# Where the GELU of a hybrid layer is evaluated: in the SSM's output stage or in the last stage

## The chip, the cores and the metric

The kernel runs on one core of one Trainium2 chip. The metric is the device time of one execution in microseconds; the median of three runs of the kernel before is 1507.56 us (1506.02 to 1509.1). Engines are called by their names in the profile: PE multiplies matrices, DVE, ACT and POOL work on tiles element by element, and DMAs are issued from the queues of ACT and SP.

## The reference, cut to what matters

```
h = rms_norm(x, norm_gain)                       # x: 1 x 2048 x 1024
q, k, v, z_attn, u_ssm, z_ssm, g = split(h @ w_in)
attn = windowed_gqa(q, k, v, ...) * silu(z_attn)
y = s5_bidirectional(u_ssm, ...)                 # 2048 x 512, 32 groups of 16 channels
y = gelu(y)                                      # 0.5*y*(1+tanh(0.79788*(y+0.044715*y^3)))
y = y * sigmoid(y @ w_glu + b_glu)
ssm = y * silu(z_ssm)
merged = sigmoid(g_attn) * (attn @ w_branch_attn) + sigmoid(g_ssm) * (ssm @ w_branch_ssm)
out = rms_norm(x + merged @ w_out, final_norm_gain)
```

## The kernel before

Every product of two fp32 matrices is done as three matmuls: each operand is split into a high part (ACT copies it to the matmul's rounded fp32) and a low part (the difference, on DVE or POOL), and high x high, low x high and high x low are added up in PSUM (`mm3`, L220 to L222). A weight tile of 128 columns comes from HBM on SP's queue (`raw`), ACT makes its high part `wh` (L163) and POOL its low part `wl` (L155).

The program has three long stretches. **The in-projections** run over blocks of 512 tokens (`BLK`), one output tile of 128 channels x 512 tokens at a time (24 matmuls over the 1024 inputs), from 25 us to 1064 us. Between their matmuls a second stream of work, the generator `chain()`, is advanced: `mm3` calls `tick()` and `turn()`, and these give the generator credit by a rate, so that it takes about 1.2 steps for each tick (`RATE2`). `chain()` first does the SSM in 8 frames of 64 channels each (`frame(i)`, from about 190 to 660 us), then the attention (to about 1005 us), and at its end prepares the last stage: `gelu_prep` of the first block (about 1020 to 1051 us), `attn_prep`, and two loads. **The last stage** (1064 to 1507 us) takes the blocks in the order 2, 3, 1, 0 (`BO`): `glu` (the product with w_glu), `branch` (the two branch products, sixteen `mm3` of 12 matmuls), `outp` (the output projection). While a branch runs, `gelu_prep` of the next block is advanced by one step for each tick.

Each engine executes its own instructions in the order in which the program issues them, and an instruction that waits holds up all behind it on its engine; a DMA issued from ACT's queue stands in ACT's order too. No table or planner sets this order: it is the order in which Python calls are made, with two delays: `later(n, f)` runs f at the n-th tick from now, and `store` puts a DMA off to the second flush, a tick later than the next one.

In a frame, `emit(i, half)` (L893 to L913) forms y for 32 channels x 2048 tokens in one PSUM tile: the matmuls of L901 need the low part `Ml` (DVE, L749), those of L905 the low part `Hl` of the states (DVE, L891). Then ACT copies the PSUM tile to `Y` (L909) and two stores put it into `yS` in HBM. Around it stand the tiles for the next frame: `U0l`, `U1l` (the split inputs, L749, needed by the matmuls of L858), `wo` (L692 to L694), `Z` (L831), and `rt`, `X` of the rotation (L867 to L870).

`gelu_prep(b, lag)` loads for each of 4 channel tiles e a 128 x 512 piece of `yS` into `yt` (L1423, on ACT's queue) and then does five instructions over four steps: Square on ACT (L1429, it reads the tile with a stride and writes it in token order), (1+s)*y on DVE (L1433), tanh on ACT (L1437), (1+t)*y on DVE (L1441) with the high part `gh` on ACT (L1442), and the low part `gl` on DVE (L1446). Tiles 0 and 1 are loaded at the start, tile 2 and 3 one step ahead of the Square that reads them. `glu` needs `gh` and `gl`.

Of the kernel before, what the change touches and what calls it, by code (L numbers as in the profile page):

```python
# [7 lines left out]
F32 = mybir.dt.float32  # L8
# [3 lines left out]
AF = mybir.ActivationFunctionType  # L12
ALU = mybir.AluOpType
# [5 lines left out]
D = 1024  # L19
KD = 8  # L20
BLK = 512
NBLK = 4
COL_Q, COL_K, COL_V, COL_ZA, COL_U, COL_ZS, COL_G = 0, 512, 640, 768, 1280, 1792, 2304
G, P, C, T = 32, 64, 16, 8
M = S // T
GB = 4
# [6 lines left out]
GELU_Q = 0.044715 ** 0.5  # L33
# [4 lines left out]
def kernel(  # L38
# [10 lines left out]
    V, A, Q, PE = nc.vector, nc.scalar, nc.gpsimd, nc.tensor  # L49
# [6 lines left out]
    def scratch(name, shape):  # L56
        if dbg and name in dbg:
            return dbg[name]
        return dram.tile(shape, F32, name=name)

    uS = scratch("uS", [512, T, M])
    yS = scratch("yS", [512, T, M])
# [15 lines left out]
    stg = h_pool.enter_context(tc.tile_pool(name="stg", bufs=4))  # L78
# [3 lines left out]
    def bank(tag):  # L82
        return ps.tile([128, 512], F32, tag=tag, name=tag, bufs=PSB[tag])
# [3 lines left out]
    def store(dst, src):  # L87
        stores.append((1, dst, src))
# [8 lines left out]
        stores[:] = keep  # L97

    HALF = "half"
    sides = []  # L100
    laters = []

    def later(n, f):
        laters.append((n, f))
# [10 lines left out]
    def turn():  # L115

        for sd in sides:
# [3 lines left out]
            while sd["credit"] > 0.0:  # L121
                try:
                    sd["credit"] -= 0.5 if next(sd["gen"]) is HALF else 1.0
                except StopIteration:
# [544 lines left out]
    def ssm(pool):  # L669
# [95 lines left out]
        def chan(t, g):  # L765

            return bass.AP(tensor=t.tensor, offset=t.offset + g * C * T * M, ap=[[M, T], [T * M, C], [1, M]])
# [125 lines left out]
        def emit(i, half):  # L893
            s = st[i]
            H = s["H"][0]
            pt = bank("s1")
            for j in range(2):
                g = half * 2 + j
                o = pt[:, j * M:(j + 1) * M]
                for m, (a, b) in enumerate(((0, 0), (0, 1), (1, 0))):  # L900
                    PE.matmul(o, s["M"][a][:, g], s["U"][half][b][:, j], start=m == 0, stop=False)  # L901
                for n in range(2):
                    for m, (a, b) in enumerate(((0, 0), (0, 1), (1, 0))):
                        w = s["ws"][n][a][:, g].rearrange("p j c -> p (j c)")
                        PE.matmul(o, w, H[b][:, j, n], start=False, stop=n == 1 and m == 2)  # L905
                if j == 0:
                    yield
            Y = stg.tile([128, BLK], F32, tag="st", name="Y")
            A.activation(Y, pt, AF.Copy)  # L909
            for j in range(2):  # L910
                store(chan(yS, i * GB + half * 2 + j), Y[:, j * M:(j + 1) * M])

        def frame(i):  # L913

# [48 lines left out]
            yield from slot()  # L963
            yield from slot()
            yield from emit(i, 0)
            yield from slot()
            high_h(i, 1)
# [5 lines left out]
            if nx:  # L973
                prep_o(nx, V)
                split_u(nx, 0)
            yield from slot()
            yield from emit(i, 1)
            if nx:
                split_u(nx, 1)
# [47 lines left out]
    def attention(pool, order):  # L1027
# [173 lines left out]
        for i in range(NU + 3):  # L1201
            u0, u1, u2 = unit(i), unit(i - 1), unit(i - 2)
            for m in range(6):
# [37 lines left out]
                if end is not None:  # L1241
                    end()
                yield HALF


    with tc.manual_schedule():
# [133 lines left out]
        def chain():  # L1380
            with tc.tile_pool(name="sp", bufs=1) as sp:
                yield from ssm(sp)
            prm_pool.close()
            with tc.tile_pool(name="ap", bufs=1) as ap:
                yield from attention(ap, order)
            open_final()
            yield from gelu_prep(BO[0], 0)
            yield from attn_prep(BO[0], 0)
            load_zs(BO[0], 0)
            load_zs(BO[0], 1)  # L1390


        GC = 0.7978845608028654
        fin = {}

        def open_final():
# [7 lines left out]
        def ftile(shape, dt, tag, name, bufs=1):  # L1404
            return fin["fp"].tile(shape, dt, tag=tag, name=name, bufs=bufs)
# [7 lines left out]
        gx, ax, sx, mx = {}, {}, {}, {}  # L1413

        def gelu_prep(b, lag):
            gx[b] = [ftile([128, 4, BLK], F32R, t, t) for t in ("gh", "gl")]
            gh, gl = gx[b]
            tl = {}

            def ld(e):  # L1420
                t = ftile([128, D], F32, "xr", "yt", 3)
                y = t[:, 0:BLK].rearrange("p (j m) -> p j m", j=T)
                A.dma_start(out=y, in_=yS[e * 128:(e + 1) * 128, :, b * 64:(b + 1) * 64])  # L1423
                ta = t[:, BLK:D]
                tl[e] = (y.rearrange("p j m -> p m j"), ta, ta.rearrange("p (m j) -> p m j", j=T))

            def g0(e):
                yv, ta, tav = tl[e]
                A.activation(tav, yv, AF.Square, scale=GELU_Q)  # L1429

            def g1(e):
                yv, ta, tav = tl[e]
                V.scalar_tensor_tensor(tav, tav, 1.0, yv, ALU.add, ALU.mult)  # L1433

            def g2(e):
                yv, ta, tav = tl[e]
                A.activation(ta, ta, AF.Tanh, scale=GC)  # L1437

            def g3(e):
                yv, ta, tav = tl[e]  # L1440
                V.scalar_tensor_tensor(tav, tav, 1.0, yv, ALU.add, ALU.mult)  # L1441
                A.activation(gh[:, e], ta, AF.Copy)  # L1442

            def g4(e):
                yv, ta, tav = tl.pop(e)
                V.tensor_tensor(gl[:, e], ta, gh[:, e].bitcast(F32), ALU.subtract)  # L1446

            def g12(e):
                g1(e)
                g2(e)  # L1450

            steps = (g0, g12, g3, g4)
            ld(0)
            ld(1)
            for _ in range(1 + lag):
                yield
            for k in range(13):
                for s_ in range(3, -1, -1):
                    e, r = divmod(k - s_, 3)
                    if r == 0 and 0 <= e < 4:  # L1460
                        steps[s_](e)
                yield
                if k in (4, 7):
                    ld((k - 4) // 3 + 2)

        def attn_prep(b, lag):
            ax[b] = [ftile([128, 4, BLK], F32R, t, t) for t in ("ah", "al")]
# [216 lines left out]
        for i, b in enumerate(BO):  # L1684
            nxt = BO[i + 1] if i + 1 < NBLK else None
            if nxt is not None:
                sg = add_side(gelu_prep(nxt, 1), 1.0)
            branch(b, nxt)
            if nxt is not None:
                drain(sg)  # L1690
            load_xr(b, 0, A)
            if nxt is not None:
                glu(nxt)
                sa = add_side(attn_prep(nxt, 1), 1.0)
            outp(b, nxt is None)
            if nxt is not None:
                drain(sa)
# [48 lines left out]
```

## Time and profile before

| what | value |
|---|---|
| median of the runs | 1507.56 us |
| the profiled execution's own time | 1508.19 us |
| span of the profile | 1506.4 us |
| busy: PE / DVE / ACT / POOL | 94% / 69% / 44% / 42% of the span |
| granted clock of PE, mean | 0.979 of full speed |

The profiled execution took 0.63 us more than the median, and 1.8 us of its time lie outside the span. PE is the engine with the least idle time: 1418.1 of 1506.4 us. A time of the whole can change only where PE stands still, or where it runs at the lower clock, or where PE is not the engine that ends last. The waits of PE, by the instruction that ended them, are therefore the first view to read; then, for each, what the engine that ended the wait had been doing. A figure in brackets at the end of a row of the timeline is the idle time of that engine just ahead of the instruction, with what ended it. Idle time of an engine other than PE is room that further work can fill.

### The profile page before, as it was taken

To read this page: it belongs to the slowest core of one execution; us is meant where nothing else is said; L and a number is where in the kernel's file an instruction comes from. 1 tells how busy PE (TensorE), PEld (TensorE's weight loads), DVE (VectorE), ACT (ScalarE), POOL (GpSimd) and SP (SyncE) were. 2 spreads that over 40 slices of the span, in tenths; PEclk is the share of its full clock that TensorE was granted. 3 is DMA by queue.
4 is the path that set the end of the run, shared out by engine and by line. 5 is a ranking of instruction groups with operands and counts; after the bars stand their busy time and mean duration, and the time that the engine had idled before them with its cause. 6 is when DMAs were issued, how large, how long until landed. Compare 5 with 4: busy or idle time off the path is not lost.

```text
span 1506.4 us, 19697 instructions
## 1 busy us (share of the span) xinstructions
PE 1418.1 (94%) x6933; PEld 1154.6 (77%) x6933; DVE 1041.8 (69%) x1954; ACT 659.9 (44%) x1213; POOL 637.9 (42%) x683
## 2 busy tenths in 40 slices
PE   7999779899999999899999999999988999999998
PEld 6787567777778777788888888888766877877886
DVE  2327977779788788647999998874577386385442
ACT  6332133433534444535666666754453243242111
POOL 5520187758678777622111111112376153252320
PEclk9999989989999999999999999999999999999999
DMA  8534222322332332554333333235776375375441
GB/s 264 157 98 95 64 81 72 100 91 76 113 105 88 109 105 88 152 175 127 92 91 92 101 96 91 90 102 148 211 212 193 98 196 181 114 182 166 117 122 70
DMA packets 240723, 185.47 MB, mean 123 GB/s; under 512 B 57921, under 2 KB 202433, under 8 KB 240625
## 3 DMA queue, kind: packets, MB, share of 16 engines
q10 hardware_dynamic: 118192, 107.89, 24.3%
q1 hardware_dynamic: 122432, 76.34, 17.1%
q8 instruction: 54, 0.88, 0.2%
q14 instruction: 45, 0.36, 0.1%
HBM read 126.56 MB, written 57.62 MB: 122 GB/s over the span
## 4 chain that ended last, share of the span: by engine, by line
PE 39%; DVE 26%; issue 7%; DMA 6%; ACT 5%; POOL 4%; ACTq 1%; DVEq 0%; POOLq 0%; SPq 0%
PE pj L220 7%; PE pj L222 7%; PE pj L221 7%; PE s L1592 3%; PE s L1593 3%; PE s L1594 3%; DVE Hl L891 2%; DMA yt<-yS 2%; DVE X L879 2%; PE s L1163 2%; DVE X L868 2%; PE s L1110 2%; DVE rt L867 2%; DVE X L870 2%; PE s L1147 2%
## 5 line engine op out<-in xcount | busy, mean ns | idle before, releaser
L155 POOL TENSOR_TENSOR wl<-raw,wh 128x256 fp32r<-128x256 f32 x380 | 355.0, 964 | 573.5 <-ACT wh L163 483.7
L220 PE MATMUL pj<-hh,wh 128*128 128x512 f32 x976 | 391.2, 401 | 0.0
L222 PE MATMUL pj<-hh,wl 128*128 128x512 f32 x976 | 385.7, 395 | 0.0
L221 PE MATMUL pj<-hl,wh 128*128 128x512 f32 x976 | 385.6, 395 | 0.0
L222 PEld LDWEIGHTS pj<-hh,wl 128*128 128x128 f32 x976 | 185.6, 190 | 41.0
L220 PEld LDWEIGHTS pj<-hh,wh 128*128 128x128 f32 x976 | 186.3, 191 | 34.0
L221 PEld LDWEIGHTS pj<-hl,wh 128*128 128x128 f32 x976 | 186.1, 191 | 34.3
L163 ACT ACTIVATE wh<-raw 128x1024 fp32r<-128x1024 f32 x96 | 100.7, 1051 | 23.4 <-DMA raw<-in_w_branch_ssm_dram 7.9
L1592 PE MATMUL s<-woh,mh 128*128 128x512 f32 x256 | 102.3, 400 | 6.7 <-DVE xr L1599 6.7
L1594 PE MATMUL s<-woh,ml 128*128 128x512 f32 x256 | 102.0, 398 | 0.0
L1593 PE MATMUL s<-wol,mh 128*128 128x512 f32 x256 | 101.9, 398 | 0.0
L1127 ACT ACTIVATE p<-p,sml 128x384 f32<-128x384 f32 (+1 forms) x128 | 75.8, 594 | 16.3 <-DVE sml L1123 16.1
L1636 POOL TENSOR_TENSOR sm<-sm,mhalf 128x1 f32<-128x1 f32 x15 | 8.3, 550 | 170.1 <-DVE sm L1635 133.4
L404 ACT ACTIVATE st<-pj,bg 128x512 f32<-128x512 f32 x64 | 43.8, 685 | 79.0 <-PE pj L222 69.3
L1111 DVE CUSTOM_DVE_ANT_0 p<-s,bias 128x384 f32<-128x384 f32 (+1 forms) x128 | 68.3, 535 | 13.7 <-PE s L1110 13.2
L1599 DVE TENSOR_TENSOR xr<-xr,s 128x512 f32<-128x512 f32 x32 | 21.9, 686 | 69.3 <-PE s L1594 69.3
L867 DVE TENSOR_TENSOR rt<-X,es 128x1020 f32<-128x1020 f32 x32 | 43.3, 1353 | 38.1 <-issue 14.4
L1152 DVE TENSOR_TENSOR pl<-s,ph 128x512 fp32r<-128x512 f32 x92 | 62.9, 683 | 4.2 <-ACT ph L1150 2.9
L1110 PE MATMUL s<-kst,qs 128*128 128x384 f32 (+1 forms) x256 | 65.7, 339 | 0.0
L1592 PEld LDWEIGHTS s<-woh,mh 128*128 128x128 f32 x256 | 48.5, 189 | 20.5 <-DVE xr L1599 8.9
L870 DVE TENSOR_TENSOR X<-X,rt 128x510 f32<-128x510 f32 x64 | 62.0, 1009 | 1.1
L891 DVE TENSOR_TENSOR Hl<-X,Hh 64x1024 fp32r<-64x1024 f32 x32 | 46.7, 1460 | 17.9 <-ACT Hh L886 17.4
(307 smaller groups left out, 3049.2 us busy)
## 6 DMA issues: line engine op xcount, KB each, us to landing
raw<-in_w_in_dram SPq DMA_DIRECT2D x59, 512.0 KB
gS<-st ACTq DMA_DIRECT2D x64, 256.0 KB
gt<-gS ACTq DMA_DIRECT2D x64, 256.0 KB
x<-in_x_dram SPq DMA_DIRECT2D x16, 512.0 KB
raw<-in_w_branch_attn_dram SPq DMA_DIRECT2D x32, 256.0 KB
raw<-in_w_branch_ssm_dram SPq DMA_DIRECT2D x32, 256.0 KB
out_dram<-xr ACTq DMA_DIRECT2D x15, 512.0 KB
xr<-in_x_dram SPq DMA_DIRECT2D x12, 512.0 KB
```

The source lines that it names most:

```text
L155: eng.tensor_tensor(lo[:, ks], r[:, ks], hi[:, ks].bitcast(F32), ALU.subtract)
L163: A.activation(res[0], r, AF.Copy)
L220: PE.matmul(pt, w[0][:, k], r[0][:, k], start=start and k == 0, stop=False)
L221: PE.matmul(pt, w[0][:, k], r[1][:, k], start=False, stop=False)
L222: PE.matmul(pt, w[1][:, k], r[0][:, k], start=False, stop=stop and k == kt - 1)
L870: V.tensor_tensor(X[:, :, r], X[:, :, r], t[:, :, r], ALU.add if r == back else ALU.subtract)
L891: V.tensor_tensor(H[1][rows], xv, H[0][rows].bitcast(F32), ALU.subtract)
L1110: PE.matmul(pt[:, 0:w], s["qs"][:, h], kst[:, r, kv, k0 * 128:k1 * 128], start=r == 0, stop=r == 1)
L1127: A.activation(p[:, h, 0:w], p[:, h, 0:w], AF.Exp, bias=nm[:, j:j + 1], accum_out=den[:, j:j + 1])
L1592: PE.matmul(pt, mh[k][:, ts_], wo[0, n][:, k], start=k == 0, stop=False)
L1593: PE.matmul(pt, mh[k][:, ts_], wo[1, n][:, k], start=False, stop=False)
L1594: PE.matmul(pt, ml[k][:, ts_], wo[0, n][:, k], start=False, stop=k == KD - 1)
```

## The change

`emit` now evaluates the GELU's body on its contiguous tile: beside the copy to `Y`, ACT squares the PSUM tile into a second tile `th` (from the pool of two that the projections' tanh uses too); one tick later DVE forms (1+s)*y (`poly`), at the next tick ACT the tanh, at the third DVE (1+t)*y (`put`), and then the two stores are put off as before, so they are issued three ticks later than before. `gelu_prep` keeps the load, the split into `gh` (ACT) and `gl` (DVE), which now read the loaded tile with a stride in and out, and drops Square, the two DVE instructions and tanh. It has five steps instead of thirteen; in the branches (`lag` of 1) each step lasts two ticks. Tiles 2 and 3 are now loaded directly ahead of the step that copies them.

```
--- before.py
+++ after.py
@@ -97,6 +97,7 @@
         stores[:] = keep
 
     HALF = "half"
+    GC = 0.7978845608028654
     sides = []
     laters = []
 
@@ -906,9 +907,21 @@
                 if j == 0:
                     yield
             Y = stg.tile([128, BLK], F32, tag="st", name="Y")
+            ta = stg.tile([128, BLK], F32, tag="th", name="th", bufs=2)
             A.activation(Y, pt, AF.Copy)
-            for j in range(2):
-                store(chan(yS, i * GB + half * 2 + j), Y[:, j * M:(j + 1) * M])
+            A.activation(ta, pt, AF.Square, scale=GELU_Q)
+
+            def poly():
+                V.scalar_tensor_tensor(ta, ta, 1.0, Y, ALU.add, ALU.mult)
+
+            def put():
+                V.scalar_tensor_tensor(Y, ta, 1.0, Y, ALU.add, ALU.mult)
+                for j in range(2):
+                    store(chan(yS, i * GB + half * 2 + j), Y[:, j * M:(j + 1) * M])
+
+            later(1, poly)
+            later(2, lambda: A.activation(ta, ta, AF.Tanh, scale=GC))
+            later(3, put)
 
         def frame(i):
 
@@ -1390,7 +1403,6 @@
             load_zs(BO[0], 1)
 
 
-        GC = 0.7978845608028654
         fin = {}
 
         def open_final():
@@ -1413,6 +1425,7 @@
         gx, ax, sx, mx = {}, {}, {}, {}
 
         def gelu_prep(b, lag):
+
             gx[b] = [ftile([128, 4, BLK], F32R, t, t) for t in ("gh", "gl")]
             gh, gl = gx[b]
             tl = {}
@@ -1421,47 +1434,25 @@
                 t = ftile([128, D], F32, "xr", "yt", 3)
                 y = t[:, 0:BLK].rearrange("p (j m) -> p j m", j=T)
                 A.dma_start(out=y, in_=yS[e * 128:(e + 1) * 128, :, b * 64:(b + 1) * 64])
-                ta = t[:, BLK:D]
-                tl[e] = (y.rearrange("p j m -> p m j"), ta, ta.rearrange("p (m j) -> p m j", j=T))
-
-            def g0(e):
-                yv, ta, tav = tl[e]
-                A.activation(tav, yv, AF.Square, scale=GELU_Q)
-
-            def g1(e):
-                yv, ta, tav = tl[e]
-                V.scalar_tensor_tensor(tav, tav, 1.0, yv, ALU.add, ALU.mult)
-
-            def g2(e):
-                yv, ta, tav = tl[e]
-                A.activation(ta, ta, AF.Tanh, scale=GC)
-
-            def g3(e):
-                yv, ta, tav = tl[e]
-                V.scalar_tensor_tensor(tav, tav, 1.0, yv, ALU.add, ALU.mult)
-                A.activation(gh[:, e], ta, AF.Copy)
-
-            def g4(e):
-                yv, ta, tav = tl.pop(e)
-                V.tensor_tensor(gl[:, e], ta, gh[:, e].bitcast(F32), ALU.subtract)
-
-            def g12(e):
-                g1(e)
-                g2(e)
-
-            steps = (g0, g12, g3, g4)
+                tl[e] = y.rearrange("p j m -> p m j")
+
+            def chunks(t, e):
+                return t[:, e].rearrange("p (m j) -> p m j", j=T)
+
             ld(0)
             ld(1)
             for _ in range(1 + lag):
                 yield
-            for k in range(13):
-                for s_ in range(3, -1, -1):
-                    e, r = divmod(k - s_, 3)
-                    if r == 0 and 0 <= e < 4:
-                        steps[s_](e)
+            for k in range(5):
+                if k < 4:
+                    A.activation(chunks(gh, k), tl[k], AF.Copy)
+                if k > 0:
+                    V.tensor_tensor(chunks(gl, k - 1), tl.pop(k - 1), chunks(gh, k - 1).bitcast(F32), ALU.subtract)
                 yield
-                if k in (4, 7):
-                    ld((k - 4) // 3 + 2)
+                if lag:
+                    yield
+                if 0 < k < 3:
+                    ld(k + 1)
 
         def attn_prep(b, lag):
             ax[b] = [ftile([128, 4, BLK], F32R, t, t) for t in ("ah", "al")]
```

The instructions of PE, POOL and SP stand in the same order as before. On ACT, at the end of the chain (the last in-projections, `gelu_prep` of block 2; `st` and `gS` are those projections' outputs, `wh` the next weights), there stood before:

```order
L1423 DMA yt<-yS 128x8x64 x2
L404 ACTIVATE st<-pj,bg_91 128x512
L1429 ACTIVATE yt<-yt 128x512
L1437 ACTIVATE yt<-yt 128x512
L94 DMA gS<-st 128x512
L1442 ACTIVATE gh<-yt 128x512
L404 ACTIVATE st<-pj,bg_91 128x512
L1429 ACTIVATE yt<-yt 128x512
L163 ACTIVATE wh<-raw 128x1024 x2
L1437 ACTIVATE yt<-yt 128x512
```

And in the same place of ACT's order now (line numbers have moved by one to thirteen):

```order
L1436 DMA yt<-yS 128x8x64 x2
L405 ACTIVATE st<-pj,bg_91 128x512
L1448 ACTIVATE gh<-yt 128x512 x2
L94 DMA gS<-st 128x512
L1436 DMA yt<-yS 128x8x64
L1448 ACTIVATE gh<-yt 128x512
L405 ACTIVATE st<-pj,bg_91 128x512
L1436 DMA yt<-yS 128x8x64
L1448 ACTIVATE gh<-yt 128x512
L164 ACTIVATE wh<-raw 128x1024 x2
L94 DMA gS<-st 128x512
```

The two `wh` copies stood behind the copy and the Square of the first two tiles; now they stand behind all four `gh` copies and behind two loads, each with the copy that reads it right after it.

On DVE, in frame 2 of the SSM, between the low parts of the states (`Hl`) and of the next frame's inputs (`U0l`), there stood before:

```order
L401 SCALAR_TENSOR_TENSOR st<-th,pj 128x512 x2
L891 TENSOR_TENSOR Hl<-X,Hh 64x1024 x2
L401 SCALAR_TENSOR_TENSOR st<-th,pj 128x512
L692 TENSOR_TENSOR rt<-wo_re,cc_re 128x512
L693 TENSOR_TENSOR rt<-wo_im,cc_im 128x512
L694 TENSOR_TENSOR wo_3400<-rt 128x512
L692 TENSOR_TENSOR rt<-wo_re,cc_im 128x512
L693 TENSOR_TENSOR rt<-wo_im,cc_re 128x512
L694 TENSOR_TENSOR wo_3401<-rt 128x512
L749 TENSOR_TENSOR U0l<-U0l,U0h 128x512
L749 TENSOR_TENSOR U1l<-U1l,U1h 128x512
```

And now:

```order
L915 SCALAR_TENSOR_TENSOR th<-th,Y 128x512
L892 TENSOR_TENSOR Hl<-X,Hh 64x1024 x2
L402 SCALAR_TENSOR_TENSOR st<-th,pj 128x512
L918 SCALAR_TENSOR_TENSOR Y<-th,Y 128x512
L693 TENSOR_TENSOR rt<-wo_re,cc_re 128x512
L694 TENSOR_TENSOR rt<-wo_im,cc_im 128x512
L695 TENSOR_TENSOR wo_3423<-rt 128x512
L693 TENSOR_TENSOR rt<-wo_re,cc_im 128x512
L694 TENSOR_TENSOR rt<-wo_im,cc_re 128x512
L695 TENSOR_TENSOR wo_3424<-rt 128x512
L750 TENSOR_TENSOR U0l<-U0l,U0h 128x512
L750 TENSOR_TENSOR U1l<-U1l,U1h 128x512
```

`poly` of the frame's first half (L915) now stands directly ahead of `Hl`, and its `put` (L918) ahead of the six instructions for `wo` and of `U0l`. Frame 5 has the same order; in frames 0, 3, 4 and 6 the `put` stands behind `U0l`. The second half's `poly` and `put` stand behind `U1l`, with the `put` ahead of the next frame's scan.

## Rows read from the trace of the kernel before

**Rows 1.** Busy part of the page: busy us, share of span, instructions.
```profile
PE 1418.1 (94%) x6933; PEld 1154.6 (77%) x6933; DVE 1041.8 (69%) x1954; ACT 659.9 (44%) x1213; POOL 637.9 (42%) x683
```

**Rows 2.** Windows: us; busy PE, PEld, DVE, ACT, POOL; PEclk; DMA; GB/s.
```profile
235.00:600.00 365.00, 343.50 (x1904) 282.62 (x1903) 299.74 (x298) 158.93 (x255) 267.10 (x248) 0.98 0.30 95
1090.00:1140.00 50.00, 43.81 (x171) 33.07 (x170) 39.13 (x42) 24.95 (x34) 40.66 (x43) 0.93 0.77 210
1197.00:1245.00 48.00, 47.07 (x200) 36.91 (x198) 34.91 (x42) 22.05 (x29) 25.69 (x29) 1.00 0.71 176
```

**Rows 3.** Waits of PE, 180 to 700 us: total, times, longest.
```profile
PE s L901 <- DVE Ml L749: 11.7, 6, 4.0
PE s L858 <- DVE U0l L749: 7.0, 6, 1.6
PE s L905 <- DVE Hl L891: 3.7, 2, 3.5
```

**Rows 4.** Waits of PE, 1065 us to the end.
```profile
PE s L1592 <- DVE xr L1599: 6.7, 5, 2.4
PE pj L221 <- DVE gl L1446: 4.5, 3, 1.6
PE pj L220 <- ACT wh L163: 3.2, 3, 1.7
PE pj L220 <- ACT st L404: 1.7, 1, 1.7
```

**Rows 5.** One line each for its instructions: count, ns min/median/max, first and last start.
```profile
L909 ACT ACTIVATE Y<-s x16: 576/598/602, 248.4 to 661.1; 128x512 f32<-128x512 f32 x16
...
L1521 DVE SCALAR_TENSOR_TENSOR ta<-ta,g x16: 692/1038/1046, 1073.4 to 1370.8; 128x512 f32<-128x512 f32 x16
...
L1433 DVE SCALAR_TENSOR_TENSOR yt<-yt x16: 1056/1094/1640, 1030.4 to 1345.3; 128x512 f32<-128x512 f32 x16
```

**Rows 6.** Timeline of DVE, frames 1 and 2: start, us, engine, line, operation, idle before.
```profile
271.90 1.44 DVE L867 TENSOR_TENSOR rt<-X,es 128x1020 f32<-128x1020 f32 x1 [2.06 <-ACT X L860]
...
290.79 0.69 DVE L401 SCALAR_TENSOR_TENSOR st<-th,pj 128x512 f32<-128x512 f32 x1 [2.80 <-ACT th L400]
...
316.23 0.69 DVE L401 SCALAR_TENSOR_TENSOR st<-th,pj 128x512 f32<-128x512 f32 x1 [3.19 <-ACT th L400]
...
375.08 3.10 DVE L891 TENSOR_TENSOR Hl<-X,Hh 64x1024 fp32r<-64x1024 f32 x2 [0.25 <-ACT Hh L886]
```

**Rows 7.** Timeline of DVE, later in frames 2 and 3.
```profile
391.38 1.22 DVE L867 TENSOR_TENSOR rt<-X,es 128x1020 f32<-128x1020 f32 x1 [3.81 <-issue]
...
456.95 0.36 DVE L831 SCALAR_TENSOR_TENSOR Z<-eye,dd,Z 128x16 f32<-128x16 f32 x1 [2.94 <-ACT Z L830]
```

**Rows 8.** Windows table, two stretches at the lower clock.
```profile
301.90:305.30 3.40, 3.40 (x13) 2.82 (x12) 3.40 (x4) 0.00 (x0) 3.40 (x4) 0.50 0.02 5
1073.30:1076.70 3.40, 3.40 (x10) 2.63 (x9) 2.61 (x4) 2.16 (x4) 1.95 (x3) 0.50 0.76 238
```

**Rows 9.** Timeline of ACT at the end of the chain.
```profile
1029.25 1.12 ACT L1429 ACTIVATE yt<-yt 128x512 f32<-128x512 f32 x1 [2.17 <-DMA yt<-yS]
...
1035.44 2.01 ACT L163 ACTIVATE wh<-raw 128x1024 fp32r<-128x1024 f32 x2
...
1037.16 0.53 ACTq L1423 DMA_DIRECT2D yt<-yS  x1
```

**Rows 10.** Timeline of PE there: first matmul of the next projection.
```profile
1037.06 0.39 PE L220 MATMUL pj<-hh,wh 128*128 128x512 f32 x1
```

**Rows 11.** Critical chain: start us, us, what.
```profile
1043.62 3.38 DMA yt<-yS
...
1336.51 6.47 DMA yt<-yS
```

**Rows 12.** Timeline of PE in the first block's branch and output.
```profile
1138.72 0.50 PE L221 MATMUL pj<-gl,wh 128*128 128x512 f32 x1 [1.40 <-DVE gl L1446]
...
1161.01 0.50 PE L1592 MATMUL s<-woh,mh 128*128 128x512 f32 x1 [1.97 <-DVE xr L1599]
```

## The prediction

> **What bounds the kernel now.** I read the busy part of the page first: PE works 1418.1 of 1506.4 us, DVE 1041.8, ACT 659.9 [rows 1]. An instruction moved between DVE and ACT stages therefore counts only where PE waits for one of these two, and the change has two such places, the SSM and the last stage. The windows say how full they are: in 235 to 600 us DVE is busy 299.74 of 365 us, ACT 158.93; in the first branch (1090 to 1140) DVE 39.13 of 50, ACT 24.95 and PE only 43.81, while in the second (1197 to 1245) PE is busy 47.07 of 48 [rows 2]. Third come PE's waits by what ended them. In the SSM they all end on DVE: 11.7 us on `Ml`, 7.0 on `U0l`, 3.7 on `Hl` [rows 3]. In the last stage they are 6.7 on `xr`, 4.5 on `gl`, 3.2 on `wh`, 1.7 on `st` [rows 4]. So about 22 us of waits stand where the change adds work, and about 16 us where it takes work away. The question is how much of either moves.
>
> **A. The SSM.** Each of 16 half frames gains a Square and a tanh on ACT and two instructions on DVE. Square reads the same PSUM tile as the copy to `Y`, whose median is 598 ns [rows 5]; I take 0.6 us for Square, and nothing for tanh, as ACT has 206 of 365 us free. The contiguous three-operand DVE instruction with two SBUF tiles that the trace has is L1521: 692 to 1046 ns, median 1038 [rows 5]. I take 1.04, because POOL is busy 267.10 of 365 us here [rows 2]; both ends are kept for the range.
> [...]
>
> What of that is on the path:
> - Frame 1, first half: the Square of frame 0's second half stands ahead of the copies to `X` for which `rt` at 271.90 already waits (idle 2.06, ended by ACT), and its `put` ahead of the scan; the chain from there over ACT's queue to the store, `Ml`, `Hh`, `th`, the `st` at 290.79 and `Hl` has no slack of its own, since the idle of 2.80 there [rows 6] ends on ACT, which waits for DVE in turn. 0.6 + 1.04 on `Ml`.
> - Frame 1, second half: Square ahead of the `th` for which `st` at 316.23 waits 3.19 [rows 6]: 0.6 on `Hl`.
> - Frame 2: `poly` ahead of `Hl`, where only 0.25 us of idle time stands at 375.08 [rows 6]: 1.04 - 0.25 = 0.8; `put` ahead of `wo` and `U0l`: 1.04. Both on `U0l`.
> - Frame 5: the same `put`: 1.04 on `U0l`.
> - All the rest at nothing: the second halves' `poly` and `put` fall into the idle times of DVE ahead of `rt` and `Z`, which are 3.81 and 2.94 us in frames 2 and 3 [rows 7] and of like size in the later ones. Where this cover is gone, each costs 1.04.
> Sum 1.64 + 0.6 + 1.84 + 1.04 = 5.1 us. After the longest wait of before, 4.0 us on `Ml` [rows 3] just ahead of 301.9 us, PE's granted clock stands at 0.50 for 3.4 us [rows 8], which costs half of these, 1.7 us. Two waits of this kind grow here, and I count one more such stretch: A = +6.8 us. Ends: +1.0, if only the `put` of frame 1 counts (below nothing is excluded, as no instruction leaves this stage); +12.5, if `poly` and `put`, 2.08 us, count in each of the 6 frames in which PE already waits [rows 3].
> `th` has two buffers, and `emit` holds one for three ticks while the projections' tanh use the same two; Y holds one of the four `st` slots three ticks longer. I cost both at nothing because an evacuation's tile is free one DVE instruction later; a projection that has to wait shows as a wait of ACT for DVE.
>
> **B. The end of the chain.** Before, the two `wh` copies begin at 1035.44 and last 2.01 us, so the first is ready at 1036.49 [rows 9]; the projection that needs it begins at 1037.06 [rows 10]: 0.57 us of slack. Now they stand behind two loads that are each followed at once by their reader. The first copy can begin where Square began, 1029.25; two copies of 0.63 us with the second tile's landing between them: about 1031.8. Then twice a load, 3.38 us to landing [rows 11], with a copy of 0.63, and one `st` of 0.67: 1031.8 + 2 x 4.0 + 0.7 = 1040.5, and 1.05 for the first `wh`: 1041.5. PE stands still for about 4.5 us, and 1.7 more go for the clock, as after the 4.0 us above. In return PE is that much later than ACT at the start of `glu`, and its wait for `st` of 1.7 us [rows 4] goes, with the stretch at half clock that follows it from 1073.3 (3.4 us, so 1.7) [rows 8]. B = 4.5 + 1.7 - 1.7 - 1.7 = +2.8 us. Ends: -3.4, if the loads land in time and both savings stand; with the longest landing, 6.47 instead of 3.38 [rows 11], 6.2 more: +9.0.
> [...]
>
> **C. The three branches.** Removed per block: 4 Squares, 4 tanh, 8 DVE instructions of about 1.1 us (L1433: median 1094 ns, strided [rows 5]). That is some 9 us of DVE in a branch of 50 in which it is busy 39 [rows 2], so the lag that DVE has at the branch's end goes: the three waits for `gl`, 4.5 us together, the first 1.40 at 1138.72; and those for `xr` in the first three blocks, 6.7 less the last block's 2.4, which has no preparation beside it: 4.3, the first 1.97 at 1161.01 [rows 4, 12]. After that last one I give back one stretch at half clock, as long as those of [rows 8]: 1.7. Against that stand six loads (two a block) that now have no lead: ACT stands from the load's issue to its landing, 3.4 to 6.5 us [rows 11], and behind it wait the weights' `wh` copies, `mh` copies and the loads of the gates. ACT is free for 26 of 48 us [rows 2], so most of this is hidden; I price each load at the mean wait for `wh` of today, 3.2 / 3 = 1.07 us [rows 4], and let today's three go: 6.4 - 3.2 = +3.2. C = -4.5 - 4.3 - 1.7 + 3.2 = -7.3 us. Ends: -13.7, if today's `wh` waits go too and no load costs anything; for the other end see the second rival.
>
> **Sum.** 6.8 + 2.8 - 7.3 = +2.3 us on the profiled run's own 1508.19: 1510.5. That run is 0.63 above the median, so 1509.9; I say 1510.
>
> **The rivals.**
> 1. *The SSM's slack takes nearly all, and the branches give back all.* For it: DVE has 65 of 365 us free in the SSM, and the DVE waits of PE there end chains which run through ACT and DMAs as well. Against: 6 waits on `Ml` [rows 3] say that DVE sets the pace in most frames. A = +1.0, B = +2.8, C without waits for loads = -4.5 - 4.3 - 1.7 = -10.5: 1508.19 - 6.7 - 0.63 = 1500.9, faster.
> 2. *The loads without lead take the gain.* Place: ACT's queue in the three branches; it decides as soon as a load's landing is longer than the stock of ready weights. For it: the longest landing is 6.47 us, a pair of weights lasts about 11 us of matmuls, and `wh` is late three times already. Against: half of ACT's time is free. Price: half of a middle landing, (3.4 + 6.5) / 4 = 2.5 us each, 15 for six, less today's 3.2, with the clock's 1.7 not given back: C = 15 - 3.2 - 8.8 = +3.0. 1508.19 + 6.8 + 2.8 + 3.0 - 0.63 = 1520, slower.
> 3. *Nothing that counts moves.* PE's order is unchanged, the added work sits in idle time, and at the end of the branches other waits take over where those for `gl` and `xr` were, since DMA is busy 0.77 and 0.71 of the time there [rows 2] and `xr` needs a load too. 1507.6.
>
> **How the numbers follow.** The forecast has 45%, its own range is 1504 to 1516; rival 1 has 28%, rival 2 18%, rival 3 9%. 0.2% is 3 us, about what a measurement of this kernel can tell from no change, so "same" is 1504.5 to 1510.6. Of the forecast's 45 I put 7 on faster, 19 on same and 19 on slower; rival 1 gives 23 and 5; rival 2 1 to same and 17 to slower; rival 3 1, 7 and 1. That is 0.31 faster, 0.32 same, 0.37 slower. The range 1498 to 1520 holds the forecast's cases, rival 3 and all of rival 1 but its far end, where C reaches -13.7, and half of rival 2; some 2 in 10 lie outside.
>
> **What the profile after would show.** A: the waits for `Ml`, `U0l` and `Hl` sum to 5 us more than 22.4, in frames 1, 2 and 5 above all; the new DVE instructions last 0.7 to 1.05; if the sum is unchanged, A is wrong. B: one wait for `wh` of 4 to 5 us near 1037, none for `st` near 1072. C: no waits for `gl`, those for `xr` only in the last block, and some new ones of about 1 us for `wh`; ACT idle ahead of the second and third `gh` copies for several us, ended by a load. The forecast is wrong as a whole if PE's waits in the branches grow by more than 10 us, or if those in the SSM do not move at all.

## The result and the profile after

The changed kernel takes 1529.01 us (median of 4 runs, 1527.12 to 1531.69) against 1508.33 of before: ratio 1.015, 95% interval [1.0134, 1.0167], 20.7 us slower. The forecast was 1510 us in a range of 1498 to 1520.

The page first: its span and busy part.

```profile
span 1525.1 us, 19720 instructions
PE 1419.7 (93%) x6933; PEld 1154.9 (76%) x6933; DVE 1033.4 (68%) x1954; ACT 656.0 (43%) x1213; POOL 639.5 (42%) x683
```

PE does the same work as before [rows 1] in 18.7 us more; PE and POOL are busier by 1.6 us each, no other engine is. So the loss is waiting. Where it arises is seen by following one instruction through both traces: the first score matmul of the attention, which follows the SSM. From the view of a single line (count, ns min/median/max, first and last start) before and after:

```profile
L1110 PE MATMUL s<-kst,qs x256: 274/337/423, 697.6 to 1002.3; 128*128 128x384 f32 x112, 128*128 128x256 f32 x16
```

```profile
L1123 PE MATMUL s<-kst,qs x256: 274/337/423, 716.2 to 1020.2; 128*128 128x384 f32 x112, 128*128 128x256 f32 x16
```

18.6 of the 18.7 us are there when the attention begins. PE's waits of after, from 180 to 700 us, answer to [rows 3]:

```profile
PE s L902 <- DVE Ml L750: 18.3, 8, 4.8
...
PE s L859 <- DVE U0l L750: 11.6, 7, 3.4
PE s L822 <- ACT wo L761: 8.3, 2, 6.3
...
PE s L906 <- DVE Hl L892: 5.4, 4, 3.1
```

The three DVE waits make 35.3 us instead of 22.4. One that I had not looked at, on `wo`, has grown to 8.3; in the trace of before the same view has

```profile
PE s L821 <- ACT wo L760: 4.0, 1, 4.0
```

From 1005 us to the end (answering to [rows 4]) there stand:

```profile
PE s L1583 <- DVE xr L1590: 8.9, 5, 2.9
PE pj L221 <- ACT wh L164: 8.4, 6, 2.4
```

The waits for `gl` and `st` are gone, as forecast; the trace of before has no others of these between 1005 and 1065 us, so the two views can be compared. But those for `xr`, which were to go in the first three blocks, have grown by 2.2 us, and those for `wh` from 3.2 to 8.4. The first branch, window of 50 us (columns as in [rows 2]):

```profile
1106.00:1156.00 50.00, 45.03 (x170) 34.62 (x171) 30.98 (x36) 18.62 (x24) 35.89 (x40) 0.90 0.77 209
```

DVE fell from 39.13 to 30.98 us of 50 there, ACT from 24.95 to 18.62, and PE still stands for 5 us. The last stage has shed the work and is no faster: from the last score matmul to the end it takes 504.9 us, 504.1 before. The new instructions themselves last about what they were priced at, except the copy to `gh`:

```profile
L912 ACT ACTIVATE th<-s x16: 587/594/606, 247.6 to 680.1; 128x512 f32<-128x512 f32 x16
...
L915 DVE SCALAR_TENSOR_TENSOR th<-th,Y x16: 676/1100/1227, 251.3 to 682.6; 128x512 f32<-128x512 f32 x16
...
L918 DVE SCALAR_TENSOR_TENSOR Y<-th,Y x16: 678/693/1219, 262.9 to 687.6; 128x512 f32<-128x512 f32 x16
...
L1448 ACT ACTIVATE gh<-yt x16: 1061/1134/1166, 1047.1 to 1354.5; 128x512 fp32r<-128x512 f32 x16
```

`gh` reads its tile with a stride now and takes 1.13 us, as the strided Square did; I had put 0.63, which is what the contiguous copy of before lasts:

```profile
L1442 ACT ACTIVATE gh<-yt x16: 615/632/634, 1033.3 to 1348.2; 128x512 fp32r<-128x512 f32 x16
```

### The profile page after: what moved, and what is told of

The parts are those of the page before. It is cut to its first block, busy times and chain, and to the rows that moved or that the text cites. A ratio compares the mean times of both kernels' runs of the same rounds, so it can differ in the third digit from the quotient of the medians.

```text
span 1525.1 us, 19720 instructions
## 1 busy us (share of the span) xinstructions
PE 1419.7 (93%) x6933; PEld 1154.9 (76%) x6933; DVE 1033.4 (68%) x1954; ACT 656.0 (43%) x1213; POOL 639.5 (42%) x683
## 4 chain that ended last, share of the span: by engine, by line
PE 39%; DVE 23%; DMA 8%; issue 7%; POOL 5%; ACT 4%; ACTq 1%; SPq 0%; DVEq 0%; POOLq 0%
PE pj L221 7%; PE pj L223 7%; PE pj L222 7%; PE s L1583 3%; PE s L1584 3%; PE s L1585 3%; DVE Hl L892 3%; POOL wl L156 2%; DMA yt<-yS 2%; PE s L1176 2%; DVE X L869 2%; PE s L1123 2%; DVE X L880 2%; DVE rt L868 2%; PE s L1160 2%
## 5 line engine op out<-in xcount | busy, mean ns | idle before, releaser
L1124 DVE CUSTOM_DVE_ANT_0 p<-s,bias 128x384 f32<-128x384 f32 (+1 forms) x128 | 68.3, 534 | 14.1 <-PE s L1123 11.2
L1547 DVE SCALAR_TENSOR_TENSOR ml<-m,mh 128x512 fp32r<-128x512 f32 x32 | 30.4, 950 | 54.3 <-ACT mh L1539 54.3
L868 DVE TENSOR_TENSOR rt<-X,es 128x1020 f32<-128x1020 f32 x32 | 43.7, 1365 | 31.7 <-POOL hl L1280 10.5
```

What stands on the lines that cost most here:

```text
L868: V.tensor_tensor(t, X[:, :, ::-1], s_, ALU.mult)
L1124: V.tensor_tensor_reduce(out=p[:, h, 0:w], in0=pt[:, 0:w], in1=bias[:, kv * 4 + h, r0:r1:-1], scale=1.0, scalar=0.0, op0=ALU.add, op1=ALU. ...
```

## The experiments

Each time is a median, beside the kernel before on the same chip (1508.25 to 1509.08 us). The code cuts are shortened: `...` stands for lines left out, and names such as `tanh` for the calls of the diff above.

**1. The halves of the change apart.** `ssm_only` is the new `emit` with the old `gelu_prep`:

```
 Y = stg.tile(...); ta = stg.tile(..., tag="th", bufs=2)   # emit as changed
 ...
 def gelu_prep(b, lag):                                     # as before
```

> The new emit (Square, tanh and the two DVE instructions, stores three ticks later) with the last stage of before, unchanged; the GELU is so applied twice. If the whole loss is made in the SSM, as the two traces say (19 of 20 us are there at 668 us), this takes 1525 to 1530 us. If the SSM costs only the 6.8 us forecast and the rest comes from the end of the chain and the branches, it takes about 1515 us.

`final_only` is the reverse:

```
-            A.activation(ta, pt, AF.Square, scale=GELU_Q)
-            later(1, poly); later(2, tanh); later(3, put)
+            store(chan(yS, ...), Y[...])                    # emit as before
```

> The emit of before with the new gelu_prep: y is loaded and split without any GELU (left out). By the two traces the last stage neither gains nor loses: 1508 to 1510 us. By the forecast's terms B and C it gains 4.5 us: about 1504 us.

Measured: `ssm_only` 1528.62 us, ratio 1.0139 [1.0113, 1.0165], +20.4 us; `final_only` 1507.75, 0.9998 [0.9985, 1.0011], -0.5 us. So the SSM costs all, and the last stage gains nothing.

**2. What costs in the SSM: engine time.** `dve_only` adds to the kernel before two DVE instructions whose result nobody reads, `act_only` two on ACT (in the very last half frame they are issued at once instead of ticks later):

```
+            later(1, lambda: V.scalar_tensor_tensor(sc, ccr, 1.0, ccr, ALU.add, ALU.mult))   # dve_only
+            later(3, lambda: V.scalar_tensor_tensor(sc, ccr, 1.0, ccr, ALU.add, ALU.mult))
...
+            A.activation(sc, pt, AF.Square, scale=GELU_Q)                                    # act_only
+            later(2, lambda: A.activation(sc, sc, AF.Tanh, scale=0.7978845608028654))
```

> The kernel before, with two more DVE instructions of the same size in each half frame, one tick and three ticks after emit, which read a constant and write a scratch tile that nobody reads: DVE's time alone, with no new wait between engines. Theory D (DVE sets the pace of the SSM, so most of its added 30 us lie on the path): 1522 to 1527 us. Theory Q (the loss comes from ACT and DVE waiting for each other: stores that wait for put, Square that waits for a th buffer, put that waits for tanh): 1510 to 1515 us.

> The kernel before, with a Square from PSUM and a tanh in each half frame on ACT, which write a scratch tile that nobody reads. Theory D: within 3 us of before. A third reading, that ACT's 19.6 us lie on the path as well, since the chains of the SSM pass through ACT: 1513 to 1520 us.

Measured: `dve_only` 1515.62, 1.0046 [1.0029, 1.0062], +7.4 us; `act_only` 1508.43, 1.0 [0.9985, 1.0015]. Theory D falls, and `dve_only` lies just above Theory Q's range: of 30 us of DVE's time some 7 are on the path (the interval is 4 to 9), and none of ACT's. Some 13 us of the 20 come from something else.

**3. What else: buffers and queues.** `store_moved` puts only the two stores of y off, in the kernel before; `late_store` puts them off further, in the changed one; `own_th` leaves the `th` buffers to the GELU alone; `own_late` does both.

```
+            later(3, put)                       # store_moved: put only calls store()
...
-                    store(chan(yS, ...), Y[...])
+                    stores.append((3, chan(yS, ...), Y[...]))        # late_store
...
-            th = stg.tile([128, BLK], F32, tag="th", name="th", bufs=2)
-            A.activation(th, pt, AF.Tanh, scale=0.5)
-            V.scalar_tensor_tensor(st, th, 1.0, pt, ALU.add, ALU.mult)
+            A.activation(st, pt, AF.Tanh, scale=0.5)                  # own_th
+            V.scalar_tensor_tensor(st, st, 1.0, pt, ALU.add, ALU.mult)
```

> The kernel before; only the two stores of y are put off by three more ticks, to where the changed kernel issues them. No GELU there, and nothing they wait for is late. Theory P (place: on ACT's queue the two issues of 0.6 us now stand ahead of the store of Z, on which the load of Ml and the Hh copies hang): 1513 to 1518 us. Theory W (wait: what costs is that they wait for put on DVE): 1507 to 1510 us.

> The changed kernel with the two stores put off by two more ticks, so that put has long been done when they stand on ACT's queue, and they stand at another place of it. Theory W: ACT's waits for put go, 1518 to 1522 us. Theory P: 1518 to 1524 if they now stand behind the store of Z, 1527 to 1532 if ahead of it. Theory B (the th buffers): no change, 1529 us.

> The changed kernel, where the projections' tanh writes the output tile itself, so that the th buffers belong to the GELU alone. Theory B (Square waits for a th buffer that put frees: 4.5 us of ACT in frame 1): 1523 to 1526 us. Theories P and W: 1528 to 1530 us.

> Both of the edits of late_store and own_th. If the couplings are the loss beyond DVE's time, and these two are they, the kernel stands where DVE's time alone puts it: 1514 to 1517 us. If not, 1520 us or more, and something else couples.

Measured: `store_moved` 1517.05, 1.0069 [1.0046, 1.0092], +8.6 us with no GELU at all; `late_store` 1520.05, 1.0081 [1.0057, 1.0104], 9.0 less than the changed kernel, which Theories P and W both allow; `own_th` 1524.45, 1.0112 [1.0085, 1.0139], 4.6 less, with an interval that overlaps the changed kernel's a little; `own_late` 1518.07, 1.0067 [1.0041, 1.0093], 2.0 less than `late_store`, which is within the noise, and a little above the expected range. Theory P stands, since in `store_moved` the data was ready. Theory W is not needed: `late_store` takes away place and wait together and gains 9.0, where the place alone costs 8.6. That W costs nothing is not shown: in the changed kernel's frame 2 the two stores go out at 382.12, just as `put` ends at 382.08. What `own_th` removes is seen on ACT in the changed kernel: the Square of frame 1's second half waits for the buffer that `put` frees, and the copy `U1h` and the loads of U stand behind it.

```profile
322.13 0.60 ACT L911 ACTIVATE Y<-s 128x512 f32<-128x512 f32 x1 [0.41 <-PE s L906]
327.20 0.60 ACT L912 ACTIVATE th<-s 128x512 f32<-128x512 f32 x1 [4.47 <-DVE Y L918]
```

That leaves whether the stores cost by their place or because `Y` is held longer. `store_behind` holds `Y` longest, and puts the stores behind the load of `Ml`:

```
-                store(chan(yS, ...), Y[...])
+                stores.append((11 if half == 0 else 7, chan(yS, ...), Y[...]))
```

> The kernel before; only the two stores of y of each half frame are put off still further, behind the load of Ml and the Hh copies (7 and 11 ticks). If their place ahead of the store of Z is what cost in store_moved: 1506 to 1511 us. If the cost is that Y holds its buffer longer, it is held longest here: 1517 us or more.

Measured: 1509.44, 1.0009 [0.9996, 1.0022]. It is the place. PE's waits for `Ml` from 235 to 660 us, first in `store_moved`, then in `store_behind` (before: 11.7):

```profile
PE s L901 <- DVE Ml L749: 17.2, 8, 4.0
```

```profile
PE s L901 <- DVE Ml L749: 11.2, 7, 4.0
```

The two timelines of ACT in frame 4, first `store_moved`, then `store_behind` (DMA rows give the time that the issue holds the queue):

```profile
458.29 1.21 ACTq L94 DMA_DIRECT2D yS<-Y  x2
459.60 0.43 ACTq L943 DMA_DIRECT2D zS<-Z  x1
...
462.32 4.49 ACTq L838 DMA_DIRECT2D Ml<-zS  x4
466.85 2.14 ACT L886 ACTIVATE Hh<-X 64x1024 fp32r<-64x1024 f32 x2 [4.65 <-DMA Ml<-zS]
```

```profile
458.42 0.33 ACTq L939 DMA_DIRECT2D zS<-Z  x1
...
461.16 0.60 ACTq L838 DMA_DIRECT2D Ml<-zS  x1
461.79 1.81 ACTq L838 DMA_DIRECT2D Ml<-zS  x3
463.65 2.14 ACT L886 ACTIVATE Hh<-X 64x1024 fp32r<-64x1024 f32 x2 [1.40 <-DMA Ml<-zS]
464.74 1.52 ACTq L94 DMA_DIRECT2D yS<-Y  x2
```

With the stores ahead, `zS` goes out 1.2 us later, and the four issues of the `Ml` load, which wait for it, hold the queue for 4.49 us instead of 2.4: `Hh` begins 3.2 us later. DVE's `Hl`, the rotation and `Ml` stand behind it, and PE waits for `Ml` in `store_moved`, while at this place it waits for nothing in `store_behind`:

```profile
476.79 0.38 PE L901 MATMUL s<-U0h,Ml 128*128 128x256 f32 x1 [2.40 <-DVE Ml L749]
```

In the changed kernel the row of `Hh` stands at 473.37, with 4.05 us of idle time, and the same wait of PE is there with 2.63 us. Why the four issues last longer with two transfers under way is not shown by any run.

**4. Why the last stage gains nothing.** `early_loads` is the changed kernel with tiles 2 and 3 loaded ahead of their reader, `final_early` the same without the GELU in `emit`; `tail_early` and `branch_early` do it at one of the two places.

```
             for k in range(5):
                 ...
+                if not lag and k < 2:       # end of the chain (tail_early)
+                    ld(k + 2)
+                if lag and 0 < k < 3:       # branches (branch_early)
+                    ld(k + 1)
                 yield
                 if lag:
                     yield
-                if 0 < k < 3:
-                    ld(k + 1)
```

> The changed kernel with the loads of tiles 2 and 3 ahead of their readers: in the branches one step (two ticks) earlier, at the end of the chain two steps. By the second rival (the loads without lead take the gain of the last stage) it gives back 3 to 7 us: 1522 to 1526 us. If the waits for xr are set by glu's own chain, as the trace after suggests, and only those for wh are made by the loads: 1525 to 1528 us.

> The emit of before with the new gelu_prep and the same earlier loads; the GELU is left out. It shows what the last stage can gain at most from the work taken out of it. Forecast's term C without its waits: 1498 to 1502 us. With the waits for xr untouched: 1503 to 1506 us.

> The changed kernel with the earlier loads at the end of the chain alone. By the trace after, where PE waits 2.3 us for wh there and stands 4.4 us later behind it: 1524 to 1527 us. By the forecast's term B, 6.2 us of loss there: 1522 to 1524 us.

> The changed kernel with the earlier loads in the three branches alone. If the branches hold most of the 18 us that early_loads gave back: 1514 to 1518 us. By the forecast's price of 1.07 us a load, six loads: 1522 to 1524 us.

Measured: `early_loads` 1511.03, 1.0015 [1.0001, 1.0029], 18.0 less than the changed kernel; `final_early` 1491.18, 0.9891 [0.9874, 0.9909], 17.4 less than before; `tail_early` 1523.06, 1.01 [1.0083, 1.0117], 6.0 less than the changed kernel; `branch_early` 1514.95, 1.005 [1.0031, 1.0069], 14.1 less. Of `early_loads` and `final_early` both readings missed: each gained more than any of them. All expectations that kept the waits for `xr` were wrong. In the changed kernel's branch one row says it: the load is issued at 1124.22, and ACT copies the tile 6.6 us later; of ACT's 8.35 us of idle time the first 1.8 lie ahead of the issue.

```profile
1124.22 0.54 ACTq L1436 DMA_DIRECT2D yt<-yS  x1
1130.79 1.07 ACT L1448 ACTIVATE gh<-yt 128x512 fp32r<-128x512 f32 x1 [8.35 <-DMA yt<-yS]
```

ACT's total wait for these loads from 1005 us to 1420, first in `final_only`, then in `final_early`:

```profile
ACT gh L1436 <- DMA yt<-yS: 49.9, 13, 8.5
```

```profile
ACT gh L1436 <- DMA yt<-yS: 22.8, 9, 5.2
```

And PE's waits from 1005 us, in the same order:

```profile
PE pj L221 <- ACT wh L164: 9.8, 7, 3.9
PE s L1571 <- DVE xr L1578: 8.9, 4, 2.9
```

```profile
PE pj L221 <- ACT wh L164: 6.4, 4, 3.4
PE s L1574 <- DVE xr L1581: 3.3, 2, 2.9
```

With early loads the waits for `xr` fall to 3.3 us: they did belong to the lag of the branches, as forecast, and a late load brings the lag back, since `mh`, and DVE's `ml` behind it, stand behind it on ACT. From 1020 to 1400 us DVE's idle time ahead of `ml` that ends on `mh` is 48.6 us in the changed kernel, 31.7 in `early_loads` and 24.4 before. PE's waits are not all of the gain. From the last score matmul to the end `early_loads` is 14.1 us shorter than the changed kernel in the two traces: 7.5 of it is idle time of PE, and 6.6 is busy time of the same 2009 matmuls, at a mean granted clock of 0.99 instead of 0.98.

**5. A version that beats both.** `t2b` has all of it: early loads, `th` for the GELU alone, the stores behind the load of `Ml`, and `poly`, tanh and `put` moved into DVE's idle time ahead of `rt`. `t3_sp` issues the stores from SP instead, three ticks earlier (`ns` of 2), `t4` leaves the DVE instructions at the changed kernel's ticks.

```
+            n1, n2, n3, ns = (4, 5, 6, 5) if half == 0 else (1, 1, 2, 5)   # t2b; t4: (1, 2, 3, 8), (1, 2, 3, 4)
+            later(n1, poly); later(n2, tanh); later(n3, put)               # put: stores.append((ns, ...))
...
-                A.dma_start(out=d, in_=s)
+                (nc.sync if d.tensor is yS.tensor else A).dma_start(out=d, in_=s)    # t3_sp
```

> The changed kernel with all that the runs so far point to: th buffers of its own, early loads, poly, tanh and put of both halves in DVE's idle time ahead of rt (four to six ticks after emit for the first half, one and two for the second), and the stores behind the load of Ml. If DVE's place and the place of the stores are the whole loss of the SSM: 1503 to 1509 us. If DVE's time costs 7 us wherever it stands: 1511 to 1515 us.

> As t2b, but the stores of y go out from SP's queue, so that ACT issues none of them. If the two issues on ACT's queue still cost at t2b's place: 1 to 4 us faster than t2b. If their place there is free: the same as t2b; slower, if the wait for put on SP's queue holds up the loads of weights.

> As t2b, but with poly, tanh and put at the ticks of the changed kernel (one, two and three after emit) and the stores still behind the load of Ml. If DVE's place is worth its 7 us: 1502 to 1506 us against 1497.7 of t2b. If DVE's time costs the same wherever it stands: 1496 to 1500 us.

Measured: `t2b` 1497.71, 0.9929 [0.9909, 0.9949]; `t3_sp` 1498.71, 0.9939 [0.9921, 0.9958]; `t4` 1500.83, 0.9944 [0.9924, 0.9964]. All three beat the kernel before by 8 to 11 us, and `t2b` is below both of its expected ranges. They are not told apart by their intervals, and `t4` lies between its two ranges, so what DVE's place is worth stays open. The profile of `t2b`:

```profile
span 1496.1 us, 19712 instructions
PE 1412.7 (94%) x6933; PEld 1151.8 (77%) x6933; DVE 1036.0 (69%) x1954; ACT 657.8 (44%) x1213; POOL 638.1 (43%) x683
```

It stands 6.5 us above `final_early`, which has no GELU. That is about `dve_only`'s 7.4 us, but there the DVE instructions stand elsewhere; that both are the same cost is not shown.

## Why the prediction was wrong

**A, the SSM: +6.8 forecast, +20.4 measured.** What was priced was priced well: the DVE instructions with one more stretch at half clock (0.50 for 3.4 us, [rows 8]) at 5.6 us, against 7.4 in `dve_only`; Square at 1.2 and tanh at nothing, where `act_only` shows none for either. That L1521's time goes with POOL, on which the choice of 1.04 rests, is seen in the trace of before: 692 to 694 ns in the six executions during which POOL stands idle, 928 to 1046 in the ten during which it works. Of the 32 new DVE instructions in the trace after the 13 with POOL idle last 676 to 693 ns; of the 19 others 15 last 1094 to 1227, four 680 to 717. The step that failed is what was costed at nothing or not at all. The two stores, which the section on the change told to be issued three ticks later, have no term in the sum: 8.6 us by `store_moved`. "I cost both at nothing" was said of the two `th` buffers and of the `st` slot that `Y` holds. For the slot it holds, as `store_behind` keeps it longest and costs nothing; the `th` buffers cost 4.6 us by `own_th`, but 2.0 by `own_late` against `late_store`, which is within the noise. With both couplings taken out `own_late` is 9.6 us above before, close to `dve_only`'s 7.4.

The terms 7.4 + 8.6 + 2.0 to 4.6 make 18.0 to 20.6, against 20.4, but the intervals of the first two are 4 to 9 and 7 to 14 us, so this is no proof that they add up. At the first score matmul the traces have 5.3 us for `dve_only` and 5.5 for `store_moved`, of 18.6 in the changed kernel: what the changes cost only together stays open, and so does the longer wait for `wo`, 5.2 us in `dve_only`. The reading that PE's waits in the SSM "all end on DVE" passed over that one, which ends on ACT.

I followed the queue of DVE past every moved instruction and did not do the same for ACT's queue and the DMAs in it.

**B, the end of the chain: +2.8.** The load term, 4.5 us of wait and 1.7 of clock, was 6.2; `tail_early` gives 6.0. That the two agree is in part luck: in the trace after PE waits 2.3 us for `wh` there, not 4.5, in the place named, and over the 4 us from 1058 the mean granted clock is 0.58, the first 3.4 of them at 0.50, which costs another 1.7: 4.0 us in all; where the other 2 come from is not shown. The copies and loads stand on ACT in the order forecast. But I added each load and its copy one after the other, 4.0 us a pair, and the rows show the second load issued 0.06 us after the copy ahead of it begins, so that from a load's issue to its copy's begin, 3.6 and 3.3 us, is all that a pair adds:

```profile
1048.51 0.53 ACTq L1436 DMA_DIRECT2D yt<-yS  x1
1052.06 1.13 ACT L1448 ACTIVATE gh<-yt 128x512 fp32r<-128x512 f32 x1 [2.84 <-DMA yt<-yS]
1052.12 0.53 ACTq L1436 DMA_DIRECT2D yt<-yS  x1
...
1055.44 1.06 ACT L1448 ACTIVATE gh<-yt 128x512 fp32r<-128x512 f32 x1 [1.67 <-DMA yt<-yS]
...
1056.40 1.99 ACT L164 ACTIVATE wh<-raw 128x1024 fp32r<-128x1024 f32 x2
```

**C, the branches: -7.3.** "I price each load at the mean wait for `wh` of today, 1.07 us" is the step that failed. Six loads cost 14.1 us by `branch_early`, 2.35 each; the second rival's price was 2.5, with the place that the runs show. Its mechanism, a landing longer than the stock of ready weights, is not what they show: from the changed kernel to `branch_early` PE's waits for `xr` fall from 8.9 to 3.8 us, and those for `wh` do not fall (8.4 and 9.8). What a late load costs is the lag of `mh` and `ml`, which I had named among what waits on ACT and then priced by `wh` alone. The savings were sized about right: 17.1 us in B and C together (1.7 + 1.7, 4.5 + 4.3 + 1.7, and today's 3.2 for `wh`) against 17.4 in `final_early`, though its trace still has 6.4 us of waits for `wh`. The savings and the loads' 6.0 + 14.1 nearly cancel; `final_only` has -0.5.

The second rival's 1520 came nearer by its price of the loads, but its last stage was +5.8 against -0.5 measured, and its SSM a third of what was measured. My range ended at the rival, with A's own upper end, 12.5 and 1.7 for the clock, not added to it.

## What to carry to other kernels

When a change moves a DMA's issue, write down what stands behind it on the queue that issues it, and behind that; two stores of 0.6 us each in every half frame cost 8.6 us in all (`store_moved`) because a store that a load waits for came next. Do the same for a load issued directly ahead of its reader on the reader's own queue: the six in the branches were issued 4.9 to 7.5 us ahead of the copy that waits for them and cost 14.1 us in all by `branch_early`, though ACT was busy only 18.62 of 50 us in the first branch. Before crediting a stage with work taken out of it, see whether what is left in it still has its lead.

## What was not expected of the hardware

The copy on ACT that reads a 128x512 tile with a stride took 1.13 us (L1448 of the changed kernel, median of 16), against 0.63 us for the contiguous one (L1442 of before). The six loads of 256 KB without lead took 4.9 to 7.5 us from their issue to the copy that reads them; in the first branch DMA is busy 0.77 of the time. The longest landing that the rows of before had shown was 6.47 us. And the issue itself was not free: in frame 4 the four issues of the `Ml` load held ACT's queue for 2.4 us behind the store of `Z` alone (`store_behind`), for 4.49 with the two stores of y ahead of it (`store_moved`).
